# Attention scores with the keys' lower parts on both halves of the partitions

## The chip, the core and the metric

The kernel runs on one core of a Trainium2 chip, as one launch. The metric is the device time of a launch in microseconds. The kernel before takes 2958.13 us, the median of 3 runs (2956.07 to 2959.81). TensorE multiplies, VectorE (DVE), ScalarE (ACT) and GpSimd (POOL) do the element-wise work, and the SP queue issues most DMAs.

## The reference, cut to what matters

One decoder layer over 2048 prompt tokens and a sample group of 8 x 4 tokens. Its input product gives, among others, queries (8 heads of 64), keys and values (2 heads of 64). The attention is windowed: 128 queries see 256 keys.

```
s = jnp.einsum('...qkgd,...skd->...kgqs', q, k).astype(jnp.float32) * (HEAD_DIM ** -0.5)
s = jnp.where(mask, s, -jnp.inf)
m = jnp.maximum(jnp.max(s, -1, keepdims=True), sink)
p = jnp.exp(s - m)
p = p / (jnp.sum(p, -1, keepdims=True) + jnp.exp(sink - m))
return jnp.einsum('...kgqs,...skd->...qkgd', p, v)
```

Beside it run a state-space branch (a scan over chunks of tokens), gates that merge the two branches, an output projection with a layer norm, and a channel mixer of width 2816 with a second layer norm. All arrays are 32-bit floats.

## The kernel before, in words

The prompt is worked off in 4 blocks of 512 tokens (`body`, L1214); block 1 also carries the 32 sample rows, and therefore splits its columns into 256 and 288. Products keep the precision of 32-bit floats with two parts per operand: an upper part in the rounded type F32R, and a lower part, the rest. A product a·b is then three products: upper·upper, lower·upper, upper·lower. A unit of the main products (`ws_unit`, L226) has a stationary weight tile of 128 columns and 512 moving token columns, 24 products with 8 slices of the input. Each unit's weights are loaded by SP (`load_to`, L188) and split into parts (`split_to`, L196: `wh` on ACT, `wl` on VectorE or, every third, GpSimd), three units ahead.

Everything else is background work (`Background`, L48): chains of small stages, of which the next is issued at each tick between two units. Each engine works off its instructions in program order, and waits for other engines by semaphores; tiles come from pools with a fixed number of buffers, of which the one named "s" holds nearly all activations (`SLOTS`, L25).

Each block computes its keys first (L1263 to L1271). `kh[h]` holds the upper part of head h's keys, the same 64 rows on both halves of the 128 partitions. `kl` is one tile: head 0's lower part on partitions 0 to 63, head 1's on 64 to 127. Column 0 to 127 of each is the window carried over from the block before (L1261). A query tile `q` (L1294) holds a head's upper part on the half of its key head, and its lower part on the other half. So the one product with `kh` over 128 rows (L883) gives (upper + lower query)·upper key, and the product with `kl` over 64 rows (L884) adds upper query·lower key.

The chain of an attention step (`attn_chain`, L869) is: `a0` the scores of 4 heads (eight products into two banks of PSUM), `a1` mask and maximum on VectorE, `a2` the exponentials on ACT, `a3` the division on GpSimd (`pp`), `a4_` the transposes back on TensorE, `a6` the products with the values (L933), `a7` their split. There are 8 chains per block, 32 in all. Between them stand the chains of the state-space branch (`ssm_chain`, L697): VectorE scans (`m`, L776), GpSimd puts together the states (`ht`), TensorE multiplies them out (L802 to L804).

Of the kernel before, what the change touches and what calls it, by code (L numbers as in the profile page):

```python
# [8 lines left out]
F32 = mybir.dt.float32  # L9
F32R = mybir.dt.float32r  # L10
# [14 lines left out]
SLOTS = 62  # L25
# [22 lines left out]
class Background:  # L48
    """Work that is issued in small steps between the units of the main products."""
# [6 lines left out]
    def add(self, at, fn, order=0):  # L56
        """What takes results out of PSUM goes before what fills more of it."""
        self.todo.append((self.now + at, -order, self.n, getattr(fn, "fills", False), fn))
        self.n += 1
# [20 lines left out]
def tile_hybrid_layer(ctx: ExitStack, tc: tile.TileContext,  # L80
# [48 lines left out]
    # ------------------------------------------------------------------ weights  # L129
# [53 lines left out]
    class Weights:  # L183
# [23 lines left out]
        def ahead(self):  # L207
            """The next split, once the products of the unit before the last are all issued."""
            self.load_to(self.pos + 4)
            self.split_to(self.pos + 3)  # L210
# [15 lines left out]
    def ws_unit(hi, lo, kk, xh, xl, cols, psl=None, late=False, part=(0, None)):  # L226
        """Weights [128, kk, 128] stationary; activations [128, n] moving, for each range of columns."""
        psl = psl or [P() for _ in cols]
        ops = [(k, w, x) for k in range(kk) for w, x in ((hi, xh), (hi, xl), (lo, xh))]
        if late:  # the activations' lower parts come last  # L230
            ops = ([(k, hi, xh) for k in range(kk)] + [(k, lo, xh) for k in range(kk)]
                   + [(k, hi, xl) for k in range(kk)])
        for i, (k, w, x) in list(enumerate(ops))[part[0]:part[1]]:
            for ps, (c0, n) in zip(psl, cols):
                T.matmul(ps[:, :n], w[:, k, :], x[k][:, c0:c0 + n], start=(i == 0), stop=(i == len(ops) - 1))  # L235
        return psl
# [6 lines left out]
    def sample_mm(ps, a, wh, wl, first, last):  # L243
        """The sample's 32 rows: a holds their upper parts, then their lower parts, whose product has rows of its own."""
        if last:
            T.matmul(ps[:32], a[:, 0:32], wl, start=False, stop=False)
        T.matmul(ps[:64], a, wh, start=first, stop=last)
        if not last:
            T.matmul(ps[:32], a[:, 0:32], wl, start=False, stop=False)

    def wide(n):
        """The sample's parts for n products, [128, 64] each."""
        t = [S("sp", 512, F32R) for _ in range((n + 7) // 8)]
        return [t[k // 8][:, (k % 8) * 64:(k % 8) * 64 + 64] for k in range(n)]

    # ------------------------------------------------------------------ constants
# [14 lines left out]
    # keys: each head's upper part on both halves of the partitions, and the lower parts  # L271
    kh = [const.tile([128, 640], F32R, name=f"kh{i}") for i in range(2)]
    kl_ = const.tile([128, 640], F32R, name="kl")
    for t in kh + [kl_]:
        ts(t[:, 0:128], jp, 0.0)
# [12 lines left out]
    # per-channel vectors: conv_w (j f), conv_b, ln1_g, ln1_b  # L288
# [20 lines left out]
    # ------------------------------------------------------------------ state-space tables  # L309
# [8 lines left out]
    def cmul(o_re, o_im, a_re, a_im, b_re_, b_im_, t1, t2, eng=V, neg_im=False):  # L318
        """o = a * b; t1 and t2 are scratch; with neg_im the imaginary part is negated."""
        tt(t1, a_re, b_re_, OP.mult, eng)  # L320
        tt(t2, a_im, b_im_, OP.mult, eng)
        tt(o_re, t1, t2, OP.subtract, eng)
        tt(t1, a_re, b_im_, OP.mult, eng)
        tt(t2, a_im, b_re_, OP.mult, eng)
        tt(o_im, t1, t2, OP.add, eng)

    def ssm_tables():
        """The state-space branch's tables: a list of (tick, step)."""
        # what is loaded
# [18 lines left out]
        # the powers for the state's way out (1 to 4) and for the input's way in (3 to 1), each twice  # L348
# [36 lines left out]
        def c_transposed():  # L385
# [8 lines left out]
            # C transposed, by pairs of groups, each half in its own columns: [128 (g p), 16, 2, 16]  # L394
# [16 lines left out]
        def parameters():  # L411
# [26 lines left out]
            # the quadrant q = n mod 4 in -2..2  # L438
# [21 lines left out]
            # the conjugate of the unit factor of four steps  # L460
# [10 lines left out]
            # the factor of B  # L471
# [14 lines left out]
            # B-bar, by pairs of groups, each half in its own columns: [128 (g p), 16, 2, 16]  # L486
# [12 lines left out]
        def first_phases():  # L499
            # the first chunks' phases, by doubling, of all groups  # L500
            w = S("w")
            G.tensor_copy(seed[:, 0, :, 0], E_.re)
            G.tensor_copy(seed[:, 1, :, 0], E_.im)
            m = 1
            while m < 16:
                u1, u2 = (w[:, i * 128:i * 128 + 16 * m].rearrange("p (a k) -> p a k", a=16) for i in range(2))
                top = lambda r: seed[:, r, :, m - 1:m].to_broadcast([128, 16, m])
                cmul(seed[:, 0, :, m:2 * m], seed[:, 1, :, m:2 * m], seed[:, 0, :, 0:m], seed[:, 1, :, 0:m],
                     top(0), top(1), u1, u2, eng=G)
                m *= 2  # L510

        def tile_steps(ct):
# [18 lines left out]
            def into():  # L531
                # the input's way into the state after the chunk
# [10 lines left out]
            def out():  # L543
                # the state's way out
                D.cw = [S("cw"), S("cw")]
                cwv = [x.rearrange("p (a t c) -> p a t c", t=4, c=16) for x in D.cw]
                cmul1(cwv[0], cwv[1], cm + [cneg], pw2, 4, D.s.rearrange("p (a s c) -> p a s c", s=4, c=16), neg_im=True)
                for r, nm in enumerate(("cr", "ci")):
                    made[nm, ct] = D.cw[r]
                    bg.add(2, lambda d=tabs[nm, ct], t=D.cw[r]: SP.dma_start(d, t))  # L550

            @fills
            def products():
# [8 lines left out]
                # the input's way to the output of the same chunk  # L562
# [27 lines left out]
            def phases():  # L590
                # the chunks' phases, by doubling
# [30 lines left out]
    # ------------------------------------------------------------------ block-wise parts  # L622
# [5 lines left out]
    def x_load(B, halves=(0, 1)):  # L628
        """Starts the loads of a block's rows."""
# [13 lines left out]
    def x_quarter(B, q):  # L643
        """Starts the loads of a quarter of the first block's channels."""
# [9 lines left out]
    def warm_up(n):  # L654
        """Products that nothing uses, while the tensor engine would wait for the first rows."""
# [4 lines left out]
    def x_split(B, k):  # L660
        """Channels k of a block, transposed and split."""
# [18 lines left out]
    def split(B, src, scale=None, name="z", own=None):  # L680
        """An array's upper and lower part, of a [128, n] tile; own: where the sample's go."""
# [14 lines left out]
    # ---- state-space branch, by tiles of 128 channels  # L696
    def ssm_chain(B, ct):  # L697
# [19 lines left out]
        def s0():  # L717
# [4 lines left out]
            # the prompt's chunks of each pair of groups, then the sample's  # L722
# [10 lines left out]
        na = 1 if B.sp else 2  # pairs of groups in a bank  # L733
# [82 lines left out]
        def s6():  # L816
            C.yk = S("yk")
            act(C.yk.rearrange("p (t g c) -> p g t c", t=4, c=16), C.y.rearrange("p (g t c) -> p g t c", t=4, c=16))
            if B.sp:
# [4 lines left out]
                # the state after the sample's steps  # L824
# [43 lines left out]
    # ---- attention, by blocks of 128 queries and key heads  # L868
    def attn_chain(B, qb, kv):  # L869
        C = Blk()  # L870
        r0 = 64 * kv
# [5 lines left out]
        def a0():  # L877
            C.s = [P(), P()]
            for j in range(4):
# [4 lines left out]
                T.matmul(o, q[r0:r0 + 64], kl_[r0:r0 + 64, ks], start=False, stop=True)  # L884
# [64 lines left out]
    # ---- the sample group's own parts  # L949
    def sample_consts(B):  # L950
# [11 lines left out]
        # masks over 128 cached and 32 new keys, rows (b, j, t)  # L962
# [167 lines left out]
    # ---- layer norms on rows of tokens  # L1130
# [6 lines left out]
    def ln_stats(B, i):  # L1137
        """Mean and deviation of rows: scale and bias of the normalisation."""
# [51 lines left out]
    def ln2_last(B, i):  # L1190
        """The norm of the last rows: as little as possible after their last product."""
# [10 lines left out]
    # ------------------------------------------------------------------ the blocks  # L1202
# [11 lines left out]
    def body(B, nxt):  # L1214
        n, cols = B.n, B.cols
        segs = [(i, c0, min(c, 512 - c0)) for i, (c0, c) in enumerate(cols)]  # the prompt's columns

        # ---- the state-space input, rows of every fourth token
# [33 lines left out]
        # ---- keys, values, queries  # L1252
# [6 lines left out]
        if B.b:  # L1259
            for t in kh + [kl_]:  # L1260
                V.tensor_copy(t[:, 0:128], t[:, 512:640])  # L1261
            V.tensor_copy(vt[:, 0, :], vt[:, 4, :])
        ps = full(("k",))  # L1263
        for i, c0, c in segs:
# [4 lines left out]
            for h in range(2):  # L1269
                r = slice(64 * h, 64 * h + 64)  # L1270
                tt(kl_[r, sl], ps[i][r, 0:c], kh[h][r, sl].bitcast(F32), OP.subtract)  # L1271
# [22 lines left out]
        def query(j):  # L1294
            ps = full(("q", j))
            # a head's upper part where its keys are, its lower part on the other half of the partitions
# [23 lines left out]
        # ---- the branches' gates and the state-space branch's way out  # L1320
# [53 lines left out]
        # ---- the attention branch's way out and the merge  # L1374
# [39 lines left out]
        # ---- output projection and the first layer norm  # L1414
# [146 lines left out]
        # ---- the channel mixer  # L1561
# [4 lines left out]
        def ffn_tail(f, pa, meanwhile):  # L1566
            """From the first product to h; the sample's columns follow the prompt's."""
# [37 lines left out]
        def first_units():  # L1605
            """Four units by halves of the tokens: the second half's rows are normalised under the first half's."""
# [135 lines left out]
    def last_states():  # L1742
        """The prompt's last states, and the sample group's."""
# [92 lines left out]
```

## Time and profile before

| | |
|---|---|
| median of 3 runs | 2958.13 us (2956.07 to 2959.81) |
| span of the profiled execution, from its first to its last instruction | 2955.1 us |
| what the median has above that span | 3.0 us |
| TensorE busy | 2890.1 us, 98% |
| VectorE, ACT, GpSimd busy | 57%, 39%, 35% |
| mean granted clock of TensorE | 0.991 |

The span is that of one execution, recorded by the hardware profiler; durations and starts below are from it. A busy TensorE is not TensorE at its peak: the end of a product is modelled, and products overlap. How many of them fit into a stretch is therefore read from the distance between their starts, not from the duration of one. "64\*128" behind a product is its form on the array, rows by columns.

### The profile page before, as it was taken

The numbers are of one execution on the slowest core, as the hardware profiler recorded it, in microseconds if no ns is written. First come the engines' busy times: TensorE is split into PE (matmuls) and PEld (weight loads), VectorE is DVE, ScalarE is ACT, GpSimd is POOL, SyncE is SP. The second block draws the span as 40 slices with busy tenths as digits, with TensorE's granted clock in tenths as the row PEclk, the third lists the DMA queues.
The fourth block names the chain that finished last, engine by engine and source line by source line (L and its number), as shares of the span: only waits on it lengthen the run. The fifth ranks groups of instructions, "written<-read, shape, count | busy, mean of one in ns | idle before, by whom it ended". The sixth has DMA issues, their size and how long they took to land.

```text
span 2955.1 us, 39229 instructions
## 1 busy us (share of the span) xinstructions
PE 2890.1 (98%) x15168; PEld 2437.9 (82%) x15168; DVE 1691.1 (57%) x2664; ACT 1143.2 (39%) x1991; POOL 1045.0 (35%) x1098
## 2 busy tenths in 40 slices
PE   9899999999999999999999999999999999999998
PEld 8777888888888988989978778888888777888887
DVE  7974676254574456644646743673445853576355
ACT  4335344243325425433424442442343253344241
POOL 1945154121454213521216641351114642243122
PEclk9999999999999999999999999999999999999999
DMA  4422333334622242222335224233344413323232
GB/s 137 147 61 67 119 93 103 94 93 138 186 65 79 75 130 65 87 92 80 104 103 175 85 71 143 72 100 103 89 136 149 131 58 109 106 86 107 90 94 97
DMA packets 415117, 304.30 MB, mean 103 GB/s; under 512 B 52283, under 2 KB 351122, under 8 KB 414914
## 3 DMA queue, kind: packets, MB, share of 16 engines
q1 hardware_dynamic: 412114, 293.84, 32.6%
q0 software_dynamic: 2816, 7.96, 0.8%
q8 instruction: 119, 1.95, 0.3%
q14 instruction: 68, 0.56, 0.1%
HBM read 285.30 MB, written 17.39 MB: 102 GB/s over the span
## 4 chain that ended last, share of the span: by engine, by line
PE 84%; POOL 6%; DVE 6%; issue 2%; ACT 1%; DMA 0%; SPq 0%; POOLq 0%; DVEq 0%; ACTq 0%
PE ps L235 53%; PE ps L239 8%; PE ps L241 8%; PE ps L240 8%; PE ps L286 2%; POOL w L121 1%; POOL m L121 1%; PE ps L884 1%; PE ps L883 1%; PE ps L933 1%; DVE m L121 1%; POOL ht L121 1%; DVE wl L121 1%; DVE m L776 1%; DVE x1l L121 1%
## 5 line engine op out<-in xcount | busy, mean ns | idle before, releaser
L121 POOL TENSOR_TENSOR wl<-wr,wh 128x1024 fp32r<-128x1024 f32 x144 | 358.0, 2486 | 1006.2 <-ACT wh L113 953.7
L113 ACT ACTIVATE wh<-wr 128x1024 fp32r<-128x1024 f32 x448 | 470.3, 1051 | 292.6 <-PE ps L241 195.1
L235 PE MATMUL ps<-x1l,wh 128*128 128x512 f32 (+2 forms) x1856 | 568.8, 341 | 2.5 <-DVE x1l L121 2.5
L235 PE MATMUL ps<-x1h,wh 128*128 128x512 f32 (+2 forms) x1856 | 568.7, 342 | 0.1
L235 PE MATMUL ps<-x1h,wl 128*128 128x512 f32 (+2 forms) x1856 | 567.3, 341 | 0.0
L121 DVE TENSOR_TENSOR wl<-wr,wh 128x1024 fp32r<-128x1024 f32 x304 | 395.4, 1303 | 235.6 <-ACT wh L113 234.7
L235 PEld LDWEIGHTS ps<-x1l,wh 128*128 128x128 f32 x1856 | 326.6, 188 | 44.4 <-DVE x1l L121 3.6
L235 PEld LDWEIGHTS ps<-x1h,wh 128*128 128x128 f32 x1856 | 326.4, 188 | 40.8 <-ACT x1h L115 0.3
L235 PEld LDWEIGHTS ps<-x1h,wl 128*128 128x128 f32 x1856 | 325.5, 188 | 40.8
L235 PE MATMUL ps<-xh,wh 128*128 128x512 f32 (+1 forms) x880 | 291.5, 363 | 10.8 <-DVE q L121 6.3
L235 PE MATMUL ps<-xh,wl 128*128 128x512 f32 (+1 forms) x880 | 283.4, 355 | 0.9 <-DVE wl L121 0.9
L235 PE MATMUL ps<-xl,wh 128*128 128x512 f32 (+1 forms) x880 | 284.3, 356 | 0.0
L239 PE MATMUL ps<-wh,hh 128*128 128x512 f32 x704 | 279.2, 397 | 0.0
L241 PE MATMUL ps<-wh,hl 128*128 128x512 f32 x704 | 278.2, 395 | 0.0
L240 PE MATMUL ps<-wl,hh 128*128 128x512 f32 x704 | 277.2, 394 | 0.0
L118 DVE SCALAR_TENSOR_TENSOR cv<-ae,pc,cv 128x512 f32<-128x512 f32 x176 | 145.7, 828 | 222.5 <-ACT cv L115 219.4
L235 PEld LDWEIGHTS ps<-xh,wh 128*128 128x128 f32 x880 | 159.9, 193 | 38.1 <-issue 6.9
L1572 POOL COPY cc<-ae 128x2 f32<-128x2 f32 x88 | 19.6, 223 | 467.9 <-ACT ae L113 467.0
L125 POOL TENSOR_SCALAR pp<-pp,su 128x256 f32<-128x256 f32 x128 | 140.2, 1113 | 112.2 <-ACT pt L113 47.8
L235 PEld LDWEIGHTS ps<-xh,wl 128*128 128x128 f32 x880 | 159.4, 193 | 24.3 <-DVE wl L121 1.3
L235 PEld LDWEIGHTS ps<-xl,wh 128*128 128x128 f32 x880 | 160.2, 194 | 20.7
L239 PEld LDWEIGHTS ps<-wh,hh 128*128 128x128 f32 x704 | 132.7, 189 | 30.9
(363 smaller groups left out, 4971.9 us busy)
## 6 DMA issues: line engine op xcount, KB each, us to landing
wr<-in_w_up SPq DMA_DIRECT2D x176, 512.0 KB
wr<-in_w_in SPq DMA_DIRECT2D x88, 512.0 KB
wr<-in_w_down SPq DMA_DIRECT2D x88, 512.0 KB
wr<-in_w_glu SPq DMA_DIRECT2D x64, 256.0 KB
wr<-in_w_o SPq DMA_DIRECT2D x32, 512.0 KB
xin<-in_x_prompt SPq DMA_DIRECT2D x32, 256.0 KB
wr<-in_w_in SPq DMA_DIRECT2D x32, 256.0 KB
wr<-in_w_attn_br SPq DMA_DIRECT2D x32, 256.0 KB
```

Of the source, the lines that this page charges most:

```text
L113: A.activation(out, in_, AF.Copy, scale=scale, **kw)
L118: eng.scalar_tensor_tensor(out, a, s, b, op0=op0, op1=op1, **kw)
L121: eng.tensor_tensor(out, a, b, op=op)
L125: eng.tensor_scalar(out, a, s1, None, op0=op0)
L235: T.matmul(ps[:, :n], w[:, k, :], x[k][:, c0:c0 + n], start=(i == 0), stop=(i == len(ops) - 1))
L239: T.matmul(ps[:m], ah, wh, start=first, stop=False)
L240: T.matmul(ps[:m], ah, wl, start=False, stop=False)
L241: T.matmul(ps[:m], al, wh, start=False, stop=last)
L286: T.transpose(out, in_, ident[:k, :k])
L776: V.tensor_tensor_scan(v2[:, a, r, :], r4[:, gp:gp + 1].to_broadcast([128, 128]), v1[:, a, r, :], hc[:, r, gp:gp + 1], OP.mult, OP.add)
L883: T.matmul(o, q, kh[kv][:, ks], start=True, stop=False)
L884: T.matmul(o, q[r0:r0 + 64], kl_[r0:r0 + 64, ks], start=False, stop=True)
```

## The change

`kl` becomes two tiles like `kh`: each head's lower part on both halves of the partitions. The second product of a pair then takes the whole query tile (upper and lower part) and 128 rows of keys, so it gives (upper + lower query)·lower key. The subtraction that makes the lower part is done twice per head, once for each half. To make room, the pool "s" has 61 buffers instead of 62. Docstrings and comments are dropped; since one line goes, lines behind L870 are one lower in the changed kernel.

```
-SLOTS = 62
+SLOTS = 61
...
-    kl_ = const.tile([128, 640], F32R, name="kl")
-    for t in kh + [kl_]:
+    kl = [const.tile([128, 640], F32R, name=f"kl{i}") for i in range(2)]
+    for t in kh + kl:
         ts(t[:, 0:128], jp, 0.0)
...
     def attn_chain(B, qb, kv):
         C = Blk()
-        r0 = 64 * kv
...
                 T.matmul(o, q, kh[kv][:, ks], start=True, stop=False)
-                T.matmul(o, q[r0:r0 + 64], kl_[r0:r0 + 64, ks], start=False, stop=True)
+                T.matmul(o, q, kl[kv][:, ks], start=False, stop=True)
...
         if B.b:
-            for t in kh + [kl_]:
+            for t in kh + kl:
                 V.tensor_copy(t[:, 0:128], t[:, 512:640])
...
             for h in range(2):
                 r = slice(64 * h, 64 * h + 64)
-                tt(kl_[r, sl], ps[i][r, 0:c], kh[h][r, sl].bitcast(F32), OP.subtract)
+                for o in (r, slice(64 - 64 * h, 128 - 64 * h)):
+                    tt(kl[h][o, sl], ps[i][r, 0:c], kh[h][r, sl].bitcast(F32), OP.subtract)
```

On TensorE, the first score step of block 0 (state-space products ahead of it, a gate's unit behind it), before:

```order
L804 MATMUL ps_1795<-cw_1022,ht_1705 128x128
L883 MATMUL ps_1808<-kh_87,q_1310 128x256
L884 MATMUL ps_1808<-kl,q_1310 128x256
L883 MATMUL ps_1808<-kh_87,q_1440 128x256
L884 MATMUL ps_1808<-kl,q_1440 128x256
L235 MATMUL ps_1818<-xh_166,wh_1614 128x512
```

and of the changed kernel, the same place:

```order
L804 MATMUL ps_1799<-cw_1026,ht_1709 128x128
L882 MATMUL ps_1812<-kh_87,q_1314 128x256
L883 MATMUL ps_1812<-kl_89,q_1314 128x256
L882 MATMUL ps_1812<-kh_87,q_1444 128x256
L883 MATMUL ps_1812<-kl_89,q_1444 128x256
L235 MATMUL ps_1822<-xh_168,wh_1618 128x512
```

Nothing moved on TensorE; of the pairs the first two are shown. `kl_89` is the tile of head 0. On VectorE, the keys of block 0 (two splits of weights ahead, the state-space tables behind), before:

```order
L121 TENSOR_TENSOR wl_513<-wr_447,wh_512 128x1024
L121 TENSOR_TENSOR wl_544<-wr_510,wh_543 128x1024
L121 TENSOR_TENSOR kl<-ps_516,kh_87 64x512
L121 TENSOR_TENSOR kl<-ps_516,kh_88 64x512
L121 TENSOR_TENSOR scr_203<-scr_203 128x16 x26
```

and of the changed kernel:

```order
L121 TENSOR_TENSOR wl_515<-wr_449,wh_514 128x1024
L121 TENSOR_TENSOR wl_546<-wr_512,wh_545 128x1024
L121 TENSOR_TENSOR kl_89<-ps_518,kh_87 64x512 x2
L121 TENSOR_TENSOR kl_90<-ps_518,kh_88 64x512 x2
L121 TENSOR_TENSOR scr_205<-scr_205 128x16 x26
```

Each subtraction stands there twice, and what follows on VectorE is behind it.

## Rows read from the trace of the kernel before

**Rows 1.** The page: busy time of the engines, and the chain that ended last.

```profile
PE 2890.1 (98%) x15168; PEld 2437.9 (82%) x15168; DVE 1691.1 (57%) x2664; ACT 1143.2 (39%) x1991; POOL 1045.0 (35%) x1098
...
PE ps L235 53%; PE ps L239 8%; PE ps L241 8%; PE ps L240 8%; PE ps L286 2%; POOL w L121 1%; POOL m L121 1%; PE ps L884 1%; PE ps L883 1%; PE ps L933 1%; DVE m L121 1%; POOL ht L121 1%; DVE wl L121 1%; DVE m L776 1%; DVE x1l L121 1%
```

**Rows 2.** Waits of TensorE: total us, times, longest.

```profile
PE ps L803 <- POOL ht L121: 11.7, 7, 3.3
```

**Rows 3.** Timeline, TensorE, first score step: start, us, line, tiles, form, shape.

```profile
177.04 0.36 PE L883 MATMUL ps<-kh,q 128*128 128x256 f32 x1
177.33 0.38 PE L884 MATMUL ps<-kl,q 64*128 64x256 f32 x1
...
179.52 0.51 PE L235 MATMUL ps<-xh,wh 128*128 128x512 f32 x1
```

**Rows 4.** The same, 256 columns in one form, and another change of form.

```profile
375.75 1.81 PE L235 MATMUL ps<-x1l,wh 128*128 128x256 f32 x13 [0.49 <-DVE x1l L121]
377.40 1.03 PE L286 MATMUL ps<-ident,xr 128*128 128x128 f32 x8
...
783.73 0.38 PE L286 MATMUL ps<-ident,usT 8*128 8x8 f32 x4 [0.73 <-DMA usT<-us]
784.04 0.52 PE L235 MATMUL ps<-xh,wh 128*128 128x256 f32 x2
```

**Rows 5.** The same, block 0, behind the first score step; idle before it.

```profile
190.61 0.49 PE L803 MATMUL ps<-cw,ht 128*128 128x128 f32 x2 [3.32 <-POOL ht L121]
```

**Rows 6.** A stretch: us, busy PE, PEld, DVE, ACT, POOL; granted clock, DMA share, GB/s.

```profile
864.00:868.00 4.00, 4.00 (x21) 4.00 (x21) 4.00 (x4) 0.00 (x0) 3.72 (x4) 0.57 0.00 0
```

**Rows 7.** The tile kl: count, ns min/median/max, first and last start.

```profile
L884 PE MATMUL ps<-kl,q x128: 378/381/580, 177.3 to 2426.9; 64*128 64x256 f32 x128
L121 DVE TENSOR_TENSOR kl<-ps,kh x10: 416/674/695, 50.2 to 2284.9; 64x512 fp32r<-64x512 f32 x6, 64x256 fp32r<-64x256 f32 x4
L1261 DVE CAST kl<-kl x3: 212/215/1322, 784.1 to 2280.6; 128x128 fp32r<-128x128 f32 x3
```

**Rows 8.** Timeline, VectorE, behind the keys of blocks 1, 2 and 3.

```profile
795.61 1.23 DVE L121 TENSOR_TENSOR wl<-wr,wh 128x1024 fp32r<-128x1024 f32 x1 [5.26 <-ACT wh L113]
...
1599.56 0.68 DVE L121 TENSOR_TENSOR q<-ps,q 64x512 fp32r<-64x512 f32 x1 [5.95 <-ACT q L113]
...
2291.87 1.23 DVE L121 TENSOR_TENSOR wl<-wr,wh 128x1024 fp32r<-128x1024 f32 x1 [6.24 <-ACT wh L113]
```

**Rows 9.** Block 0: timeline, a wait of TensorE; a stretch ahead of it.

```profile
126.68 0.65 PE L235 MATMUL ps<-xh,wh 128*128 128x512 f32 x1 [2.48 <-DVE q L121]
...
69.00:127.00 58.00, 53.46 (x337) 47.17 (x336) 56.69 (x81) 23.28 (x41) 54.29 (x86) 1.00 0.46 134
```

**Rows 10.** Waits of the SP queue: total us, times, longest.

```profile
SPq L708 <- POOL m L121: 14.3, 4, 6.3
```

**Rows 11.** Stretches with score steps, blocks 1 and 2; columns as in rows 6.

```profile
860.00:960.00 100.00, 99.11 (x698) 86.01 (x697) 47.46 (x136) 50.03 (x133) 42.97 (x39) 0.97 0.25 74
1643.00:1667.00 24.00, 24.00 (x129) 19.24 (x127) 21.67 (x31) 7.82 (x11) 19.93 (x22) 1.00 0.23 67
1667.00:1730.00 63.00, 63.00 (x282) 46.27 (x282) 34.25 (x90) 37.91 (x97) 27.55 (x23) 1.00 0.20 59
```

**Rows 12.** Timeline, GpSimd and TensorE, the states of blocks 2 and 3.

```profile
1662.32 2.48 POOL L121 TENSOR_TENSOR ht<-m,m 128x256 f32<-128x256 f32 x2
1664.99 0.39 PE L803 MATMUL ps<-tbcr,ht 128*128 128x128 f32 x2
...
2363.15 0.38 PE L804 MATMUL ps<-tbci,ht 128*128 128x128 f32 x1 [0.65 <-POOL ht L121]
```

**Rows 13.** Timeline, GpSimd and TensorE, the normalised scores of block 2.

```profile
1682.91 8.49 POOL L125 TENSOR_SCALAR pp<-pp,su 128x256 f32<-128x256 f32 x8
1689.21 0.39 PE L235 MATMUL ps<-xh,wl 128*128 128x512 f32 x1
1689.44 1.03 PE L286 MATMUL ps<-ident,pp 128*128 128x128 f32 x8
```

## The prediction

> **What bounds the kernel now.** The first part of the page comes first: TensorE is busy 98% of the span, the next engine, VectorE, 57% [rows 1]. Then the chain of work that ended last: its large shares are all product lines of TensorE, and the two lines of the attention scores, L883 and L884, hold 1% each, although they are only 256 of 15168 products [rows 1, 7]. Then TensorE's waits: the largest sum is 11.7 us, in 7 waits, on GpSimd's `ht` [rows 2]. So TensorE's own work sets the time almost everywhere, and what is taken from it counts, unless it then waits.
>
> Next the timeline of TensorE over one score step (eight products: four heads, upper and lower part of the keys). The first starts at 177.04, the second at 177.33, and behind the eighth the next unit's first product at 179.52: 2.48 us, 0.31 a product, while the forms alternate between 128\*128 and 64\*128 [rows 3]. Products of the same 256 columns that keep one form follow much closer: thirteen of them begin between 375.75 and 377.40, where the next group starts, 0.127 us each [rows 4], and there are as many loads of weights as products [rows 1]. Another change of form is as dear: behind four 8-row transposes that begin at 783.73 the 128-row product begins at 784.04, 0.31 us later, though the four have only 8 columns each [rows 4]. I read this as TensorE ending one product before it begins the next whenever the form changes, so that neither the stream nor the load of weights is hidden.
>
> **What the change removes.** All eight products get 128 rows of weights, so the form never changes; the order on TensorE stays, row for row. I take the distance of the thirteen, 0.125 us rounded. A step is then 8 x 0.125 = 1.00 us instead of 2.48: 1.48 less. The 128 pairs [rows 7] make 32 steps. Gross: 32 x 1.48 = 47.4 us. Bounds of the new distance: 0.115, half of what a product of 512 columns takes (0.23, 1689.21 to 1689.44 [rows 13]), if the columns alone set it; and 0.31, if the form is not the cause. I take the row with the same columns and the coming form; the lower bound would give 2.6 us more.
>
> **What it adds.** The keys' lower parts are subtracted twice instead of once: 6 more operations of 0.674 us and 4 more of 0.416, and 3 more copies of 0.215 [rows 7], together 4.0 + 1.7 + 0.6 = 6.3 us of VectorE, right behind the product of the keys (one more fill stands at the start, where TensorE has no rows yet). In blocks 1 to 3 VectorE idles soon after: 5.26 us at 795, 5.95 at 1599, 6.24 at 2291 [rows 8]; the 1.6 to 1.9 us more in each are covered there. Block 0 has no such cover: behind the keys VectorE is busy 56.7 of the 58 us from 69 to 127, and then TensorE waits for it, 2.48 us at 126.68 [rows 9]. So 2 x 0.674 = 1.35 us come on top in block 0 (bounds: 0, if the 1.3 us that are free take them up, and 1.35); if the cover in the other three were gone, 5 us more.
>
> The pool of activations has 61 buffers instead of 62. The loads on SP keep their order, but some wait for another buffer. SP's waits for buffers of the state-space tables sum to 14.3 us in 4 now [rows 10], and TensorE's list has no wait for these tables. I take 0; bounds: no gain, since nothing waits for them, and 6.3 us, the longest of the four, once uncovered.
>
> **Where the gain is not kept.** The score steps lie in four stretches, and the first part of a stretch is tight, because VectorE and GpSimd work off the state-space branch there: from 1643 to 1667, in block 2, VectorE is busy 21.7 of 24 us and GpSimd 19.9; behind that, from 1667 to 1730, 34 and 28 of 63, and TensorE all of it [rows 11]. Two steps lie in the first part, and then TensorE needs GpSimd's `ht`: in block 3 it waits for it, 0.65 us at 2363.15; in block 2 it doesn't, but the two `ht` operations that begin at 1662.32 end at 1664.80, and the first product that reads them begins at 1664.99 [rows 12]. That string doesn't get faster by the change. TensorE would be there 3.0 us earlier and wait, so 3.0 us are given back in each of the two blocks. In block 0 the first step, at 177.04, stands ahead of a wait of 3.32 us for the same kind of state, at 190.61 [rows 3, 5]: its 1.5 us go too. In block 1 VectorE has 47 of 100 us [rows 11], and I find no such place. Given back: 3.0 + 3.0 + 1.5 = 7.5 us (bounds: 0, and half of everything, as in the second rival).
>
> One more effect has both signs. The granted clock falls to 0.57 in the 4 us behind the first score step of block 1 [rows 6]. With a denser step it may stay up; a drop of that kind (the clock is at its 1.2 GHz level for most of it) costs 0.43 x 4 = 1.7 us. Against it stand new short waits: in block 2 the transposes of the normalised scores at 1689.44 read the first four of eight GpSimd operations that take 8.49 us from 1682.91, done by about 1687.2, only 2.2 us ahead [rows 13], while a unit between two steps shrinks by 1.5. I put the two at zero together.
>
> **Sum.** 47.4 - 7.5 - 1.35 = 38.5 us. The profiled execution's span is 2955.1 us; the median of the runs, 2958.13, is 3.0 above it, and that part isn't touched. Span after: 2916.6; time: 2919.6 us.
>
> **A rule that speaks against it.** The row first: products with 128 rows of weights and 256 columns follow every 0.127 us, a load for each [rows 1, 4]. The Trainium skill, "TensorE: Matmul & The Clock Gate", section "The mechanism" (packing small matmuls), says that a load of weights runs beside products in flight only when the row groups differ. By that rule loads over all rows are never hidden, the new pairs stay near 0.31 us a product, and nothing is gained. The trace doesn't bear it out for this form, so it is the third rival, with a small chance.
>
> **Rivals.**
> - *Kept in full.* VectorE's string in blocks 2 and 3 moves up too, because it waits for TensorE somewhere, and the clock stays up behind a step or two: 47.4 - 1.35 + 2.6 = 48.7, 2909 us. For it: TensorE doesn't wait in block 2 now [rows 12]. Against it: VectorE is 90% busy in that part [rows 11]. 0.11.
> - *The others become the bound.* The 63 us of block 2 become 54 by six shorter steps; VectorE's 34 and GpSimd's 28 us [rows 11] fit on average, but each stage of a chain has only one unit's time, and the slack shown is 2.2 us [rows 13]. If half of what the 24 later steps of the four blocks give (24 x 1.48 = 36 us) turns into waits, 18 are lost: 2938 us. 0.12.
> - *No gain.* The distance is that of load and stream one after the other, not of the form: VectorE's 1.35 us alone, 2959.5. Against it the thirteen products. 0.03.
> - *Slower.* One buffer fewer: SP issues its loads in one queue, and a load that waits for a buffer holds the weights behind it. Now that is 6.3 us at longest for the tables [rows 10], covered by weights that are loaded three units of 24 x 0.23 = 5.5 us ahead [rows 13]. The twelve state-space tiles of blocks 1 to 3 would each have to hold SP 38.5 / 12 = 3.2 us beyond that cover to cancel the gain; at 5 us each it is 2919.6 + 60 = 2980. For it only that the pool is shorter. 0.03.
>
> **How the numbers follow.** The forecast has 0.71; its own range is 2909 to 2929 (clock drops, 5 us of uncovered VectorE work, a few new waits). The range for 8 in 10 reaches to most of the first two rivals: 2905 to 2936. The runs of this kernel lie within 3.7 us, so about 0.2%, 6 us, can be told from no change: faster 0.71 + 0.11 + 0.12 = 0.94, within it 0.03, slower 0.03.
>
> **What would show it.** Right: the score products all have one form and start 0.12 to 0.13 us apart, a step takes 1.0 us; TensorE's waits for `ht` grow by 1.5 us at 190 and by 3 us in each of blocks 2 and 3; the six later steps of a stretch bring no new waits; the wait at 126.68 ends 1.4 us later. Wrong: a distance above 0.2 us; waits for the normalised scores of more than 10 us in all; no idle time of VectorE behind the keys in blocks 1 to 3; waits of TensorE for weights.

## The result, and the profile after

The changed kernel takes 2922.66 us (median of 4 runs, 2919.17 to 2927.61) beside 2957.10 us of the kernel before: a ratio of 0.9884 with an interval of 0.9868 to 0.9901. That is 1.2% faster. Forecast were 2919.6 us and a range from 2905 to 2936. The medians differ by 34.4 us, and the spans of the profiled executions by 35.9 (2919.2 us now); the sum had 38.5 for both.

The page after, its line of busy times (against [rows 1]):

```profile
PE 2843.7 (97%) x15168; PEld 2420.9 (83%) x15168; DVE 1697.6 (58%) x2678; ACT 1142.5 (39%) x1991; POOL 1049.9 (36%) x1098
```

The same 15168 products and loads keep TensorE busy 46.4 us less. VectorE has 14 more operations and 6.5 us more. A score step that runs wholly at full clock, timeline of TensorE (against [rows 3]; the scores stand at L882 and L883 now):

```profile
205.31 0.36 PE L882 MATMUL ps<-kh,q 128*128 128x256 f32 x1
205.51 0.28 PE L883 MATMUL ps<-kl,q 128*128 128x256 f32 x1
205.63 0.28 PE L882 MATMUL ps<-kh,q 128*128 128x256 f32 x1
...
206.23 0.28 PE L883 MATMUL ps<-kl,q 128*128 128x256 f32 x1
206.34 0.39 PE L235 MATMUL ps<-xh,wh 128*128 128x512 f32 x1
```

The eight products start 0.12 us apart, but for the first, behind which the second comes only after 0.20. From the first product of the step to the first of the next unit it is 1.03 us, where it was 2.48: 1.45 less.

The tile `kl`, all its instructions on VectorE and its products (against [rows 7]):

```profile
L883 PE MATMUL ps<-kl,q x128: 276/280/415, 182.0 to 2390.0; 128*128 128x256 f32 x128
L121 DVE TENSOR_TENSOR kl<-ps,kh x20: 416/679/695, 50.5 to 2257.2; 64x512 fp32r<-64x512 f32 x12, 64x256 fp32r<-64x256 f32 x8
L1260 DVE CAST kl<-kl x6: 213/245/1317, 776.5 to 2252.6; 128x128 fp32r<-128x128 f32 x6
```

All products have one form. There are twice the subtractions, each as long as before, and twice the copies of the window (median 245 ns beside 215).

TensorE's waits at the places that the prediction names, and the new ones (timeline of TensorE after; the idle time before a row, in us, and what ended it stand in brackets):

```profile
127.60 0.47 PE L235 MATMUL ps<-xh,wh 128*128 128x512 f32 x1 [1.69 <-DVE q L121]
...
179.06 0.49 PE L803 MATMUL ps<-cw,ht 128*128 128x128 f32 x2 [1.86 <-POOL ht L121]
...
194.37 0.80 PE L803 MATMUL ps<-cw,ht 128*128 128x128 f32 x2 [3.37 <-POOL ht L121]
...
228.32 0.66 PE L286 MATMUL ps<-ident,pp 128*128 128x128 f32 x4 [1.25 <-DVE nm L890]
...
878.30 0.40 PE L235 MATMUL ps<-xh,wh 128*128 128x288 f32 x1 [0.59 <-ACT yks L113]
...
903.90 0.52 PE L235 MATMUL ps<-xh,wh 128*128 128x256 f32 x2 [1.85 <-ACT y L113]
...
1641.63 0.49 PE L803 MATMUL ps<-tbcr,ht 128*128 128x128 f32 x2 [1.94 <-POOL ht L121]
1642.76 0.49 PE L804 MATMUL ps<-tbci,ht 128*128 128x128 f32 x2 [0.64 <-POOL ht L121]
...
2258.79 0.80 PE L744 MATMUL ps<-uP,tbxr 128*128 128x128 f32 x2 [3.73 <-ACT uP L113]
...
2321.44 0.46 PE L802 MATMUL ps<-tbtp,uP 128*128 128x128 f32 x2 [1.53 <-issue]
...
2334.26 0.49 PE L803 MATMUL ps<-tbcr,ht 128*128 128x128 f32 x2 [1.85 <-POOL ht L121]
2335.39 0.49 PE L804 MATMUL ps<-tbci,ht 128*128 128x128 f32 x2 [0.64 <-POOL ht L121]
```

The rows of before that stand against them, beside [rows 5] and [rows 12] (timeline of TensorE before):

```profile
175.32 0.49 PE L803 MATMUL ps<-cw,ht 128*128 128x128 f32 x2 [1.79 <-POOL ht L121]
...
2286.47 0.49 PE L744 MATMUL ps<-uP,tbxr 128*128 128x128 f32 x2 [2.23 <-ACT uP L113]
...
2349.21 0.46 PE L802 MATMUL ps<-tbtp,uP 128*128 128x128 f32 x2 [0.19 <-PE ps L286]
...
2362.01 0.49 PE L803 MATMUL ps<-tbcr,ht 128*128 128x128 f32 x2 [0.28 <-POOL ht L121]
```

Block 0: between the two waits that end at 179.06 and 194.37 lie 15.31 us, and 15.29 before (175.32 to 190.61); the step between them is shorter, and TensorE waits for GpSimd's string as the prediction says. The second wait itself didn't grow by the 1.5 us that the prediction names as a sign (3.37 beside 3.32), because products in this stretch ran in part at the lower clock: the step at 181.60 took 1.70 us. In e7_copy_first (below), where the same step runs at full clock (1.03 us), the wait is 4.85. Block 2: the place that had no wait [rows 12] has 1.94 + 0.64 = 2.6 us. Block 3: 1.85 + 0.64 + 1.53 where 0.28 + 0.65 + 0.19 = 1.1 stood, so 2.9; for the 1.53 the profile shows no releaser. Four rows are not in the prediction: 1.25 us at 228.32 for a maximum on VectorE, 0.59 at 878.30 for ScalarE's `yks`, 1.85 at 903.90 for its `y` (0.55 before), and 3.73 at 2258.79 for its `uP` (2.23 before). A fifth, 0.59 us at 61.90, is for a weight's lower part on VectorE. The prediction names waits for weights among the signs of being wrong; this one is part of the price of the second subtraction (e1_zero_half doesn't have it, e4_adds_only has it with 0.57). What holds `uP` is seen on ScalarE (its timeline after):

```profile
2257.97 0.28 ACT L113 ACTIVATE kx<-ps 128x128 f32<-128x128 f32 x1 [4.16 <-DVE kl L121]
2258.14 0.59 ACT L113 ACTIVATE uP<-ps 128x512 f32<-128x512 f32 x1
```

In the last block ScalarE copies keys (`kx`, L1273) out of the PSUM tile from which VectorE subtracts. The copy starts when VectorE's last `kl` is done, and `uP` is queued behind it.

TensorE's clock in block 1, behind the first step and over the 100 us of its score steps (columns as in [rows 6]):

```profile
857.00:861.00 4.00, 4.00 (x35) 4.00 (x33) 3.15 (x3) 0.27 (x1) 3.78 (x6) 1.00 0.00 0
836.00:936.00 100.00, 96.46 (x809) 90.61 (x809) 61.11 (x164) 50.52 (x135) 50.05 (x48) 1.00 0.25 76
```

The granted clock stays at its 2.4 GHz level behind the step, where it was 0.57 [rows 6], and over the whole stretch it is 1.00 where it was 0.97 [rows 11]. Not all of this is the change's doing. Two stretches of e2_slots (below), whose score steps are those of before, and one of before:

```profile
860.00:864.00 4.00, 4.00 (x33) 4.00 (x33) 3.99 (x4) 0.00 (x0) 3.78 (x5) 1.00 0.00 0
913.00:917.00 4.00, 3.85 (x18) 3.85 (x19) 3.01 (x11) 2.70 (x6) 0.00 (x0) 0.57 0.00 0
919.00:923.00 4.00, 4.00 (x22) 4.00 (x22) 3.47 (x11) 2.27 (x4) 0.00 (x0) 0.61 0.00 0
```

Behind the first step of block 1 e2_slots has 1.00 too (its first row), so the drop of [rows 6] isn't bound to the steps of before. Behind the block's fifth step both have a drop (the second row and the third).

### The profile page after: what moved, and what is told of

The parts are those of the page before. It is cut to its first block, busy times and chain, and to the rows that moved or that the text cites. A ratio compares the mean times of both kernels' runs of the same rounds, so it can differ in the third digit from the quotient of the medians.

```text
span 2919.2 us, 39248 instructions
## 1 busy us (share of the span) xinstructions
PE 2843.7 (97%) x15168; PEld 2420.9 (83%) x15168; DVE 1697.6 (58%) x2678; ACT 1142.5 (39%) x1991; POOL 1049.9 (36%) x1098
## 4 chain that ended last, share of the span: by engine, by line
PE 82%; POOL 7%; DVE 6%; issue 2%; ACT 2%; DMA 0%; SPq 0%; POOLq 0%; DVEq 0%; ACTq 0%
PE ps L235 52%; PE ps L239 8%; PE ps L241 8%; PE ps L240 8%; PE ps L286 2%; POOL m L121 2%; POOL w L121 1%; PE ps L932 1%; POOL ht L121 1%; DVE m L121 1%; DVE m L776 1%; DVE wl L121 1%; POOL wl L121 1%; PE ps L247 1%; DVE x1l L121 0%
```

## Experiments

The theory: what costs is the change between products over 128 and over 64 rows of the array, not the load of weights; the shorter steps give something back at waits for `ht`; the second subtraction costs in block 0. Rivals: every step counts in full; half of the later steps' gain turns into waits; the subtraction is covered. All eight were timed apart from the kernel after: the first four beside a before of 2956.68 us, the last four beside one of 2953.51 us. Positions are compared by the time of TensorE's first product of a known group.

**e1_zero_half**: the gain without the second subtraction. The other half of each `kl` is filled with zeros once, on GpSimd.

```
+    for h in range(2):
+        o = slice(64 - 64 * h, 128 - 64 * h)
+        for c in range(1, 5):
+            ts(kl[h][o, c * 128:c * 128 + 128], jp[o], 0.0, eng=G)
...
-                for o in (r, slice(64 - 64 * h, 128 - 64 * h)):
-                    tt(kl[h][o, sl], ps[i][r, 0:c], kh[h][r, sl].bitcast(F32), OP.subtract)
+                tt(kl[h][r, sl], ps[i][r, 0:c], kh[h][r, sl].bitcast(F32), OP.subtract)
```

What it leaves out: lower query times lower key.

> The changed kernel without the second subtraction: each head's lower key part stands on its own half of the partitions, the other half is zero from the start, so the lower query part is multiplied by zero there. All eight products of a score step keep 128 rows. Theory (the form sets the distance; the second subtraction delays VectorE in block 0): distances stay 0.12 us, a step 1.0 us; the wait on the state ahead of the second step of block 0 ends 1.4 to 3.8 us earlier than in the changed kernel, 2919 to 2921 us in all. Rival (the additions are hidden everywhere): 2922.7, and block 0 ends as in the changed kernel.

Measured: 2916.15 us, ratio 0.9860 [0.9846, 0.9873]: 6.5 us below the kernel after, more than either theory said, but the two intervals still overlap at their ends. The timeline of TensorE, e1_zero_half:

```profile
126.00 0.47 PE L235 MATMUL ps<-xh,wh 128*128 128x512 f32 x1 [1.68 <-DVE q L121]
...
2254.92 0.80 PE L748 MATMUL ps<-uP,tbxr 128*128 128x128 f32 x2 [2.30 <-ACT uP L113]
```

The first wait ends 1.60 us earlier than after (in the trace of before, which has the single subtraction too, 0.9 earlier than after), the second is 1.43 us shorter. So the second subtraction costs 1.6 us in block 0, and 1.4 us in block 3, where I had called it covered. The spans differ by 4.3 us (2919.2 and 2914.9). Of the 1.3 that are left, 0.9 stand in one wait, for VectorE's `xs` in block 1 (1.77 us at 815.14 after, 0.85 in e1_zero_half). It doesn't belong to the subtraction: e6_late_back, without the second subtraction, has 1.77 there too, and e7_copy_first, with it, 0.88. What the medians show beyond the spans is open.

**e2_slots**: the kernel before with `SLOTS = 61`, nothing else.

> The kernel before with 61 buffers in the pool of activations and nothing else. Theory (the missing buffer costs nothing): 2957 us within 3, no new waits of TensorE. Rival (a load that waits for a buffer holds the weights behind it): 2962 us or more, with new waits of TensorE for weights or tables.

Measured: 2956.96 us, ratio 0.9999 [0.9988, 1.0009]. The buffer costs nothing that can be told from noise. Waits of the SP queue in e2_slots (against [rows 10]):

```profile
SPq L708 <- POOL m L121: 16.1, 3, 7.8
```

The queue does wait 1.8 us more, and nothing comes of it. The rival that forecast 2980 us is out.

**e3_paired**: the kernel before, with the same products ordered upper, lower, lower, upper, and so on, so that the rows change four times in a step instead of eight (the way out included).

> The kernel before with the eight products of a step in another order: upper, lower, lower, upper, upper, lower, lower, upper. The 64-row products stay, but the form changes 4 times a step instead of 8. Theory (a change of rows costs, a product of 64 rows doesn't): 0.31 us at a change, 0.13 between two lower or two upper ones; a step 4 x 0.31 + 4 x 0.125 = 1.74 instead of 2.48; 32 x 0.74 = 24 us, of which about 4 are given back: 2937 us. Rival 1 (load and stream one after the other wherever the rows overlap): 0.31 also between two lower ones, which use the same 64 rows: 2.1 us a step, 2947. Rival 2 (the order doesn't matter): 2957.

Measured: 2933.13 us, ratio 0.9917 [0.9904, 0.9931]. One step on the timeline of TensorE, e3_paired:

```profile
219.17 0.36 PE L883 MATMUL ps<-kh,q 128*128 128x256 f32 x1
219.47 0.38 PE L884 MATMUL ps<-kl,q 64*128 64x256 f32 x1
219.69 0.27 PE L884 MATMUL ps<-kl,q 64*128 64x256 f32 x1
219.89 0.38 PE L883 MATMUL ps<-kh,q 128*128 128x256 f32 x1
220.11 0.28 PE L883 MATMUL ps<-kh,q 128*128 128x256 f32 x1
...
220.76 0.39 PE L883 MATMUL ps<-kh,q 128*128 128x256 f32 x1
```

Each pair of equal rows takes 0.43 us, as 0.31 + 0.12 would. But the starts don't show the expected 0.31 at a change and 0.13 inside a pair: behind the first distance they lie 0.20 to 0.23 us apart, whether the rows change or not. Where in a pair the cost arises is therefore not seen. The lower products still use 64 rows, load their weights and have 256 columns; only the number of changes fell, and the step with it: it takes 1.81 us (219.17 to 220.98) with four changes, beside 2.48 with eight before and 1.03 with none after. That is 0.17 to 0.20 us a change, so the cost goes with the changes of rows; the rival of 2.1 us a step is out. The time fell by 23.6 us, somewhat more than 32 x 0.67 = 21.4; the rest has no cause shown.

**e4_adds_only**: the kernel after, with the product on 64 rows again: all of the cost and none of the gain.

```
-                T.matmul(o, q, kl[kv][:, ks], start=False, stop=True)
+                r = slice(64 * kv, 64 * kv + 64)
+                T.matmul(o, q[r], kl[kv][r, ks], start=False, stop=True)
```

> The changed kernel with the lower product on 64 rows again, so that of the change only the second subtraction, the second tile and the 61 buffers are left. Theory: block 0 loses 1.4 us or somewhat more, because VectorE has no idle time there, the other blocks nothing: 2958 to 2961 us. Rival (all hidden): 2957. Rival (VectorE's 6.3 us count in every block): 2963.

Measured: 2959.78 us, ratio 1.0017 [1.0007, 1.0028]. With the 64 rows the gain is gone, so it comes from the rows alone. It is 2.8 us more than e2_slots, which differs only by the additions. The first place at which it falls behind is block 0 (the product at 372.62 in e2_slots starts at 374.16, 1.54 later); blocks 1 and 2 add nothing (at 1875.41 it is 1876.96, 1.55 later); then block 3, timeline of TensorE, e4_adds_only:

```profile
2285.08 0.79 PE L744 MATMUL ps<-uP,tbxr 128*128 128x128 f32 x2 [3.69 <-ACT uP L113]
```

The same wait as after, 3.69 us, where e2_slots has 2.14. It is there without the faster scores, so it comes from the subtraction alone.

**e5_early_back** and **e6_late_back**: e1_zero_half with the product on 64 rows again in five of the 32 steps each, on either side of the `ht` waits. Five full steps would cost 5 x 1.45 = 7.3 us. (The expectation of e5_early_back says the second step of block 0; what was changed is the first, at 181.60 after, the one ahead of the wait at 194.37.)

```
+                i = 2 * qb + kv
+                r = slice(64 * kv, 64 * kv + 64) if (B.b == 0 and i == 0) or (B.b > 1 and i < 2) else slice(0, 128)
+                T.matmul(o, q[r], kl[kv][r, ks], start=False, stop=True)
```

In e6_late_back the condition is `(B.b == 0 and i == 4) or (B.b > 1 and i in (3, 4))`.

> e1_zero_half with the lower product back on 64 rows in the 5 early score steps whose gain I hold to be given back at the next wait for ht (block 0: the second step, at 196 us in the kernel after; blocks 2 and 3: the first two steps). If the gain of such a step is given back, the time stays that of e1_zero_half, 2916 us, within 2 us, and TensorE's waits for ht behind these steps shrink by 1.5 to 3 us. Rival: every step counts in full: 5 x 1.48 = 7.4 us more, 2923.5 us. The traces of before and after already say about 2.6 us of the 3.0 in block 2 and 2.9 in block 3 are given back.

> The counterpart: e1_zero_half with the lower product back on 64 rows in 5 later steps (block 0: the fifth; blocks 2 and 3: the fourth and fifth). If these steps' gain is kept, 5 x 1.48 = 7.4 us more than e1_zero_half: 2923.5 us. Rival: they have waits behind them that take the gain too (the others become the bound): 2916 us, as e1_zero_half.

Measured: e5_early_back 2913.87 us, ratio 0.9867 [0.9853, 0.9880], the interval of e1_zero_half. e6_late_back 2925.17 us, ratio 0.9911 [0.9894, 0.9927], so 11.3 us more than e5_early_back beside the same runs, where 7.4 were expected; by the profiled spans it is 7.9 (2920.8 and 2912.9), and what the medians have beyond is open. From the first product of a block's first step to the last upper product of its last step:

| | block 2 | block 3 |
|---|---|---|
| e1_zero_half | 75.41 us | 77.06 us |
| e5_early_back | 75.41 us | 77.34 us |
| e6_late_back | 78.63 us | 81.92 us |

Two slow steps ahead of the `ht` wait cost next to nothing (0.0 and 0.3 us), two behind it cost 3.2 and 4.9 us (2.9 by the steps). The slow late step of block 0 doesn't count either: it stands ahead of the wait for the maximum on VectorE, 1.27 us at 225.68 in e1_zero_half, and in e6_late_back that wait is gone. Where the early ones went in block 3, timeline of TensorE, first e1_zero_half, then e5_early_back:

```profile
2317.56 0.46 PE L806 MATMUL ps<-tbtp,uP 128*128 128x128 f32 x2 [1.51 <-issue]
2330.37 0.49 PE L807 MATMUL ps<-tbcr,ht 128*128 128x128 f32 x2 [1.84 <-POOL ht L121]
```

```profile
2315.58 0.46 PE L806 MATMUL ps<-tbtp,uP 128*128 128x128 f32 x2 [0.19 <-PE ps L290]
2328.39 0.49 PE L807 MATMUL ps<-tbcr,ht 128*128 128x128 f32 x2 [0.27 <-POOL ht L121]
```

The two waits shrink by 1.32 and 1.57 us, one step each, and the 12.81 us between them stay to the hundredth, so this distance isn't set by TensorE. (What ends the first of the two waits in e1_zero_half the profile doesn't show.) The excess of e6_late_back in block 3 lies in one stretch (columns as in [rows 6]):

```profile
2330.00:2350.00 20.00, 17.66 (x86) 14.88 (x86) 11.19 (x29) 12.98 (x32) 11.77 (x11) 0.91 0.18 53
```

A granted clock of 0.91 over 20 us is 1.8 us; e1_zero_half has 1.00 there. 4.9 less 1.8 leaves 3.1, the two steps. Over its runs this kernel has a mean granted clock between 0.989 and 0.992, and times from 2922.4 to 2932.5; whether the slower scores bring the clock down is not shown by this.

**e7_copy_first**: the kernel after, with ScalarE's two copies of the keys moved ahead of the work on their upper and lower parts.

```
         ps = full(("k",))
+        if B.last:
+            kx = S("kx")
+            act(kx[:, 0:128], ps[0][:, 384:512])
+        if B.sp:
+            act(B.kvs[:, 0, :], ps[1][:, 256:288])
         for i, c0, c in segs:
...
-        if B.last:
-            kx = S("kx")
-            act(kx[:, 0:128], ps[0][:, 384:512])
-        if B.sp:
-            act(B.kvs[:, 0, :], ps[1][:, 256:288])
```

> The kernel after, with ScalarE's copy of the window's keys (kx, last block) and of the sample keys issued ahead of the work on the keys' upper and lower parts, so that it isn't queued on ScalarE behind a tile that VectorE still reads. If the second subtraction costs its time in block 3 through this queue, the wait of L744 for ACT uP there falls from 3.73 to 2.3 us or less, and the time by 1.4 to 3 us, to about 2920. Rival: the wait has another cause, or comes back elsewhere: 2922.7, as after.

Measured: 2915.66 us, ratio 0.9874 [0.9860, 0.9887]. By the ratio the kernel after would take 0.9884 x 2953.51 = 2919.2 us beside these runs, so 3.6 us less, but the two intervals overlap. The trace shows the mechanism. ScalarE, then TensorE, e7_copy_first:

```profile
2249.23 0.28 ACT L113 ACTIVATE kx<-ps 128x128 f32<-128x128 f32 x1 [1.65 <-PE ps L235]
2251.46 2.41 ACT L113 ACTIVATE kh<-ps 64x512 fp32r<-64x512 f32 x4 [1.95 <-DVE kh L1260]
2253.90 0.60 ACT L113 ACTIVATE uP<-ps 128x512 f32<-128x512 f32 x1
```

```profile
2255.02 0.38 PE L744 MATMUL ps<-uP,tbxr 128*128 128x128 f32 x2
```

The copy waits only for the product of the keys, `uP` follows the keys' upper parts directly, and TensorE's 3.73 us are gone altogether, with them the 2.23 us that the kernel before had already.

**e8_zero_copy_first**: the edits of e1_zero_half and e7_copy_first together.

> Both remedies together, the single subtraction (the other half of the partitions zeroed once) and the copy first: the candidate for the fastest version. If the copy's place matters beyond the second subtraction, 2914 us or less; if it only mattered because of the second subtraction, 2916, as e1_zero_half.

Measured: 2913.67 us, ratio 0.9869 [0.9853, 0.9884]. It has the lowest median of the versions that keep all score products on 128 rows, but its interval is that of e1_zero_half: what the copy's place brings beyond the single subtraction can't be told from nothing here, although in its trace TensorE's wait for `uP`, 2.30 us in e1_zero_half, is gone. Its profiled span is 2910.7 us, 44.4 below that of before.

## Why the prediction was right

| step | forecast, us | measured, us | from |
|---|---|---|---|
| 32 shorter steps | -47.4 | -46.4 | 32 x (2.48 - 1.03) |
| given back, block 0 | +1.5 | +1.5 | 15.29 and 15.31 us between two waits |
| given back, block 2 | +3.0 | +2.6 | new waits; e5, e6 |
| given back, block 3 | +3.0 | +2.9 | longer waits; e5, e6 |
| second subtraction, block 0 | +1.35 | +1.6 | e1 against after; 1.54 in e4 |
| second subtraction, block 3 | 0 | +1.4 | 3.73 against 2.30 in e1 |
| one buffer fewer | 0 | 0 | e2 |
| new short waits and clock | 0 | +3.1 and -2.7 | 228.32, 878.30, 903.90; block 1 at 1.00 |

The measured terms come to -36.0 us; the spans differ by 35.9. That they meet so closely is luck. Left out are the clock's drops in the other blocks, some of which lie differently in each execution, and the 0.9 us of the wait at 815.14 (0.86 us before, but 1.76 in e2_slots, so it isn't the score steps'). By the spans alone, e2_slots, which costs nothing more, is 3.6 us faster than before.

- *The distance.* Right in kind and nearly in size: 0.12 us a product, not 0.125, but the first distance of a step is 0.20, so a step takes 1.03 us. The rival without a gain is refuted, e4_adds_only shows that the gain comes from the rows alone, and e3_paired that the price goes with the changes of rows. The Trainium skill, "TensorE: Matmul & The Clock Gate", section "The mechanism", has a sentence that lets a load run beside products only when the row groups differ; by it the step would have stayed at 2.48 us. The trace doesn't agree: 0.12 us for products that all load over all rows.
- *"Whenever the form changes" was too broad.* It is the rows that count. The kernel after still changes the columns of its form among the products of the sample rows, timeline of TensorE after:

```profile
1078.78 0.40 PE L241 MATMUL ps<-wh,mgl 128*128 128x512 f32 x1
1079.01 0.40 PE L247 MATMUL ps<-wh,sp 128*64 128x512 f32 x1
1079.25 0.39 PE L249 MATMUL ps<-wl,sp 128*32 128x512 f32 x1
1079.47 0.39 PE L246 MATMUL ps<-wl,sp 128*32 128x512 f32 x1
...
1079.93 0.39 PE L239 MATMUL ps<-wh,mgh 128*128 128x512 f32 x1
```

  128\*128, 128\*64 and 128\*32 follow one another every 0.22 to 0.24 us, like products of one form. The Trainium skill, "TensorEngine Tiling (Array Packing)", section "Key Properties", says that changing the tiling mode drains TensorE. Here a change of the active rows has a price (0.17 to 0.20 us) and a change of the active columns has none; the trace shows active rows and columns, not whether a tiling mode is set.
- *Given back.* The three places and their sizes were right (7.0 us where 7.5 were forecast), and e5_early_back and e6_late_back show that a step's place decides whether it counts.
- *The second subtraction in block 0.* The place was right, the size small: 1.6 us, above the upper bound of 1.35.
- *The cover in block 3 failed.* The prediction looked for VectorE's idle time behind the keys [rows 8] and found it. The idle time is there, but a copy on ScalarE starts behind the last `kl`, and TensorE waits for what is queued behind the copy. The cover of an operation has to be looked for at its readers and at what waits for its end, not on its own engine alone. Before the change the same wait was 2.23 us long.
- *The later steps bring no new waits: not quite.* 1.25 us in block 0 and 0.6 and 1.3 us in block 1 are new, against 24 steps that gain 35. The rival in which half of that is lost is refuted.
- *The clock.* In block 1 it went as hoped, 0.97 to 1.00 over about 90 us, 2.7 us. But e2_slots and e4_adds_only, with the steps of before, need 95.0 us from block 1's first score product to the last upper product of its last step, where before needs 96.5: about 1.5 of the 2.7 belong to the execution and not to the change. Elsewhere drops came and went between executions; I put them at zero with the short waits, and the two measured sizes nearly cancel as well, which is luck and no reasoning.

## What to carry over

Short products over 128 rows and over 64 rows should not alternate: zeros or a copy in the other half, or an order that keeps equal rows together, brings back much of the time, and here the products over all 128 rows followed one another faster. Before counting a shorter step on the bound engine, look whether it stands ahead of a wait for another engine or behind the last one: ahead of it, the gain is only waiting. And before calling an instruction that is added on an idle engine covered, look whether another engine's queue waits for its end.

## What was not expected of the hardware

- Products of 256 columns that change between 128 and 64 rows each time follow every 0.31 us, and those that keep 128 rows every 0.12 us, although each loads its weights over all rows. By the length of a step a change costs 0.17 to 0.20 us. A change of the active columns costs nothing (0.22 to 0.24 us at 512 columns, as without one).
- The starts don't show where a change is paid: in e3_paired, with a change at every second product, they lie 0.20 to 0.23 us apart behind the first, at a change and without one.
- Behind the fifth score step of block 1 the granted clock fell in all four traces with lower products over 64 rows there: over 4 us it is 0.61 before, 0.57 in e2_slots and e4_adds_only, 0.58 in e3_paired. In the six traces with 128 rows it is 1.00 over the 12 us from 898 to 910, although TensorE waits longer there (1.84 to 1.86 us for `y`, beside 0.47 to 1.15). Why is open. The drop behind the block's first step is not of this kind: of the four traces only before has it.
